# Two-layer hybrid decoder: the 64-row second score product and the 40-row bias broadcast on all 128 rows

## The chip, the cores and the metric

The program runs on one core of a Trainium2 chip, in one launch. Its metric is the device time in microseconds. Three runs of the kernel before took 1497.88, 1500.16 and 1502.87 us, so the median is 1500.16 us. Engines in the profile: PE is the matrix engine (its weight loads are shown apart, as PEld), DVE the vector engine, ACT the scalar engine, POOL the general engine, SP issues most DMAs.

## The reference, cut to what matters

The model is a trunk of two layers over 512 tokens of 1024 features in float32. Each layer has a mixer, a cross-attention into 256 memory tokens and a squared-ReLU MLP, each behind a norm and with a residual sum. The mixers hold three kinds of causal attention with heads of 64 features:

```python
# layer 0: forgetting attention, 8 heads
sc = einsum("bqhd,bkhd->bhqk", q, k) * 64 ** -0.5
bias = c[:, :, q0:q1, None] - c[:, :, None, :q1]        # c: running sum of log forget gates
p = softmax(where(mask, sc + bias, -inf)); out = p @ v
# layer 1: dilated attention, 8 heads, and sliding-window attention with sinks, 8 heads over 2 key heads
sc = einsum("nbqhgd,nbkhd->nbhgqk", qb, kb) * 64 ** -0.5 # only keys at allowed distances
num, m, den = p @ v, max(sc), sum(p)                     # then joined, divided by den
```

## The kernel before, in words

Activations lie with features on the 128 partitions and the 512 tokens in columns. To keep float32 accuracy every operand of a matmul is split in two: a first part, rounded by ACT into the type float32r, and the exact rest, which DVE gets by subtraction (hi_lo). A projection is then three matmuls for each block of 128 by 128 weights: first by first, first by rest, rest by first (mm3, lines 177 to 179). Weights come in chunks of 128x1024 by DMA, are split by ACT and DVE (lines 156 and 157) and are used once.

For the three causal attentions two heads share a tile of 128 features: head hh has rows 64 hh to 64 hh + 63. q_parts gives, for each head, a tile with the first part of q on the head's own rows and the rest of q on the other 64 rows. k_parts gives, for each head, a tile with the first part of k on both halves, and one tile for both heads with the rest of k, each head's on its own rows (line 385). A block of 128 queries then takes two products into one bank: the first (line 425) contracts over 128 rows and gives both parts of q by the first part of k; the second (line 426) contracts over the head's own 64 rows only and adds the first part of q by the rest of k.

The blocks of a head are done from the last to the first: 512, 384, 256 and 128 keys; in the window attention 256, 256, 256 and 128. Layer 0 adds a third product there, a mask on the diagonal block (line 428, bfloat16), and needs for each head the row of running sums on every partition: a product of a column of a selection matrix with the tile ch, which has the sums' first part on rows 0 to 7 and their rest on rows 32 to 39, 40 rows in all (line 683), copied out by ACT. So there are 96 second score products and 8 such broadcasts.

Behind the scores soft() runs: DVE adds the bias and finds the maximum (line 339), ACT takes the exponential and the sum (342), DVE the reciprocal (347), POOL scales (348). PE transposes the blocks (354), ACT and DVE split them (156, 157), and PE multiplies with V (448, 449).

The order of PE's instructions is written by merge(): the steps of the heads (scores of one head between the products with V of the one before) and the steps of projections, as filler, go into one list by their weight on PE and by estimates of when their inputs are ready. A score's weight there counts columns, not rows. The framework then places the buffers and adds the waits. Each pool gives a fixed number of buffers by tag: the tags acth and actl have eight each, and hold the gates and outputs of the layer 0 recurrence, the attention outputs and the rest of k, which takes one from either pool by turns.

Of the kernel before, what the change touches and what calls it, by code (L numbers as in the profile page):

```python
# [9 lines left out]
F32 = mybir.dt.float32  # L10
# [13 lines left out]
# columns of the small per-feature parameters  # L24
# [12 lines left out]
def build(ctx, tc, a):  # L37
# [53 lines left out]
    # the first weights come between the first blocks of x  # L91
# [15 lines left out]
    # the table of functions loads while the first data come  # L107
# [4 lines left out]
    # A step: (its weight on TensorE, function that emits it, what it needs, what it gives). merge() puts lists of  # L112
    # steps into one order: `ready` estimates when what a step gives can be used.
# [17 lines left out]
    def merge(*lists):  # L131
        """Each list stays in its order; of the steps that are ready goes the one whose list is furthest behind."""
        tot = [max(sum(s[0] for s in x), 1e-9) for x in lists]
        at = [0] * len(lists)
        done = [0.0] * len(lists)
        while True:
            left = [i for i in range(len(lists)) if at[i] < len(lists[i])]
            if not left:
                return
            when = {i: max([0.0, *(ready.get(x, 1e9) for x in lists[i][at[i]][2])]) for i in left}  # L140
            can = [i for i in left if when[i] <= now[0]]
            if can:
                i = min(can, key=lambda i: (done[i] + 0.5 * lists[i][at[i]][0]) / tot[i])
            else:
                i = min(left, key=lambda i: when[i])
                assert when[i] < 1e8, lists[i][at[i]][2]
            s = lists[i][at[i]]
            at[i] += 1
            done[i] += s[0]
            emit(s)  # L150

# [1 line left out]
    def hi_lo(hi, lo, src, scale=None):  # L153
        """src -> hi (12 bits) + lo (the exact rest)."""
        if scale is None:
            A.activation(out=hi, in_=src, func=AF.Copy)  # L156
            V.tensor_tensor(out=lo, in0=src, in1=hi.bitcast(F32), op=ALU.subtract)  # L157
        else:
            A.activation(out=hi, in_=src, func=AF.Copy, scale=scale)
            V.scalar_tensor_tensor(out=lo, in0=src, scalar=scale, in1=hi.bitcast(F32),  # L160
                                   op0=ALU.mult, op1=ALU.subtract)

    def chunk(src):
        """1024 columns of weights: the two parts."""
        cnt[0] += 1
        i = cnt[0]
        started.append(i)
        with tc.high_priority(100 if len(started) > 4 else 0):
            raw = wp.tile([128, 1024], F32, tag="wr", name=f"wr_{i}", bufs=2)
            h = wp.tile([128, 1024], F32R, tag="wh", name=f"wh_{i}", bufs=3)  # L170
            lo = wp.tile([128, 1024], F32R, tag="wl", name=f"wl_{i}", bufs=3)
            SY.dma_start(out=raw, in_=src)
            hi_lo(h, lo, raw)
        return h, lo
# [6 lines left out]
    def proj(src, xs, after, n=S, ks=range(8), need=(), give=(), bank=None):  # L181
        """Steps for one block of 128 output features; xs: list (filled by then) of (hi, lo) by block of the
        contraction. after(ps) follows the last."""
# [15 lines left out]
    def proj2(src, xs, k0, afters, need=(), banks=None):  # L199
        """A chunk with two blocks of output features; contraction over blocks k0 .. k0 + 3."""  # L200
        st = {}

        def f(e, k):
            def g():
                if "w" not in st:
                    st["w"] = [c.rearrange("p (e k m) -> p e k m", e=2, k=4) for c in chunk(src)]
                if k == 0:
                    st[e] = (banks[e] if banks else pmm)()
                h, lo = st["w"]
                x = xs[k0 + k]  # L210
                mm3(st[e], h[:, e, k, :], lo[:, e, k, :], x[0], x[1], k == 0, k == 3)
                if k == 3:
                    afters[e](st[e])
            return g

        return [step(0.65, f(e, k), need[k] if need else ()) for e in range(2) for k in range(4)]

    def proj_v(srcs, xs, out, nb, store, give=()):
        """By token: V of 512 features for nb blocks of tokens; store(b, ps) -> out"""
# [28 lines left out]
    class Stats:  # L248
        """The root of the mean square by token, of 8 blocks of features added one by one."""
# [25 lines left out]
        def last(self, src, c):  # L275
            """The last block's squares of columns c"""
# [8 lines left out]
        def rstd(self, b0=0, nb=None, more=()):  # L285
            """[128, nb], token = (b0 + b) * 128 + p; more: parts of squares of these tokens"""
# [17 lines left out]
    def spread(r, nb=4):  # L304
        """values by token -> the same row on every partition (PSUM)"""
# [29 lines left out]
    def soft(p, i, ps, bias, dens, sink=None):  # L335
        """scores (PSUM, unscaled) + bias -> exp(scores - max), and its sum"""
# [13 lines left out]
    def to_pt(blocks, n):  # L350
        """blocks: (source block [128, 128], column) -> transposed, in two parts"""
# [7 lines left out]
    def v_parts(t, src, scale=None):  # L359
        """Heads of 64 features -> for each its two parts side by side"""  # L360
# [4 lines left out]
    lows = [0]  # L365

    def q_parts(f):
        """Two heads on rows 0-63 and 64-127 -> for each a tile with both of its parts, the first on its own rows"""
# [7 lines left out]
    def k_parts(f):  # L376
        """For each head a tile with its first part twice; and the second parts"""
        x = (t2k("qkh", F32R), t2k("qkl", F32R))
        lows[0] += 1
        lo = t2k("acth" if lows[0] % 2 else "actl", F32R)  # L380
        for hh in range(2):
# [3 lines left out]
            V.tensor_tensor(out=lo[own, :], in0=f[own, :], in1=x[hh][own, :].bitcast(F32), op=ALU.subtract)  # L385
        return (*x, lo)
# [3 lines left out]
    def evac_head(y, hh, ps):  # L390
        """Rows 0-63 plus rows 64-127 -> rows hh * 64 .. of y"""
# [9 lines left out]
    class Head:  # L401
        """One head of causal attention on rows hh * 64 .. of the pair tiles: its steps."""
# [10 lines left out]
        def score(self, i):  # L413
# [6 lines left out]
            rows = slice(64 * self.hh, 64 * self.hh + 64)  # L420
# [4 lines left out]
            T.matmul(ps[:, :w], lhsT=q[hh][:, qc], rhs=k[hh][:, ks], start=True, stop=False)  # L425
            T.matmul(ps[:, :w], lhsT=q[hh][rows, qc], rhs=k[2][rows, ks], start=False, stop=self.mask is None)  # L426
# [26 lines left out]
        def steps(self, prev):  # L453
            """Its scores, between the previous head's products with V"""
# [29 lines left out]
    def out_half(src, ys, half, then=None, need=(), late=None):  # L484
        """hT += the half of the projection that belongs to ys[4 * half:]; a list of steps for each 2 blocks"""
# [10 lines left out]
    class Both:  # L496
        """Two lists of four as one, filled later"""
# [7 lines left out]
    def out_late(src, ys, half, gname, gi, hg, st):  # L505
        """The half whose last block comes late: (what can go before it, the rest)"""
# [10 lines left out]
    def mixer0():  # L517
# [12 lines left out]
        # softplus(-lam) = max(-lam, 0) + log1p(exp(-|lam|))  # L530
# [51 lines left out]
        def recur():  # L582
            for b in range(4):
                A.activation(out=gs[b], in_=gs[b], func=AF.Gelu_apprx_tanh)
            # a = exp(-8 r sp), kept as 1 - (1 - a): 1 - a = tanh(4 r sp) (1 + a); 1 - a^2 = (1 - a)(1 + a)
# [27 lines left out]
        # forget gates: rows 0-7 take the weights' first part, rows 8-15 the rest  # L613
# [37 lines left out]
        ch = cst.tile([40, S], F32R, tag="chdm", name="ch")  # L651
        G.memset(ch.bitcast(F32), 0.0)
        self_ = cst.tile([40, 8], F32, name="self")
        sel = cst.tile([40, 8], F32R, name="sel")
# [25 lines left out]
        def bias(head):  # L680
            def f():
                ps = psc()
                T.matmul(ps, lhsT=sel[:, head:head + 1].to_broadcast([40, 128]), rhs=ch, start=True, stop=True)
# [69 lines left out]
    Rm = cst.tile([128, MEM], F32, name="Rm")  # L753

    def mem_tiles():
        """The blocks of features, one after another"""
# [202 lines left out]
    def finish(src, hid, st):  # L959
        """The last block of features, half of the tokens after half, and the final norm"""  # L960
# [22 lines left out]
    def mixer1(hg, st):  # L983
# [39 lines left out]
        def rope(c, name, need=()):  # L1023
            """Its steps, and the step after the exchange of rows by DMA"""
# [6 lines left out]
        def v_proj(c, dst):  # L1031
            """V of 128 features: by feature, then transposed; its parts -> dst, a list of tiles"""
# [30 lines left out]
        # sliding window with sinks; a pair tile holds heads p and p + 4  # L1063
# [91 lines left out]
def _by_col(w):  # L1155
    """[1024, n] -> n/128 chunks [128, 8 * 128]: partition = row within a block of 128"""
# [4 lines left out]
def _by_row(w):  # L1161
    """[1024, 512] -> 4 chunks [128, 2 * 512]"""
# [3 lines left out]
def _by_half(w):  # L1166
    """[1024, 1024] -> 8 chunks [128, 2 * 4 * 128]: a half of the rows, two blocks of columns"""
# [7 lines left out]
def _consts():  # L1175
# [12 lines left out]
    sel = np.zeros((40, 8), np.float32)  # L1188
# [74 lines left out]
```

## Time and profile before

| | us |
|---|---|
| median of three runs | 1500.16 (1497.88 to 1502.87) |
| span of the profiled execution | 1501.8 |
| PE busy | 1472.9 |
| DVE busy | 873.2 |
| ACT busy | 673.3 |
| POOL busy | 158.6 |

The page gives the profiled execution by its span, from the first to the last instruction; it names no other time for it. Busy is the time in which at least one instruction of the engine ran. Matmuls overlap each other, so PE's busy time says that it hardly rests and not how fast it goes: for that one reads the distance from the start of one matmul to the start of the next in the timeline. The three causal attentions lie from about 110 to 215 us (layer 0) and from about 776 to 955 us (layer 1).

### The profile page before, as it was taken

The numbers are of one execution on the slowest core, as the hardware profiler recorded it, in microseconds if no ns is written. First come the engines' busy times: TensorE is split into PE (matmuls) and PEld (weight loads), VectorE is DVE, ScalarE is ACT, GpSimd is POOL, SyncE is SP. The second block draws the span as 40 slices with busy tenths as digits, with TensorE's granted clock in tenths as the row PEclk, the third lists the DMA queues.
The fourth block names the chain that finished last, engine by engine and source line by source line (L and its number), as shares of the span: only waits on it lengthen the run. The fifth ranks groups of instructions, "written<-read, shape, count | busy, mean of one in ns | idle before, by whom it ended". The sixth has DMA issues, their size and how long they took to land.

```text
span 1501.8 us, 18306 instructions
## 1 busy us (share of the span) xinstructions
PE 1472.9 (98%) x6912; PEld 1201.5 (80%) x6912; DVE 873.2 (58%) x1507; ACT 673.3 (45%) x1161; POOL 158.6 (11%) x172
## 2 busy tenths in 40 slices
PE   8999999999999999999999999999999999999996
PEld 5777777888888888888877777788888888888885
DVE  7786767555444444444568887766454444444543
ACT  3776654444431323324446866645343323142342
POOL 3002212000200000000212221300021000000002
PEclk9999999999999999999999999999999999999998
DMA  5222213432333333233232222144323333233331
GB/s 192 80 82 71 71 56 120 141 112 72 98 98 99 98 94 97 92 98 98 98 105 78 63 72 84 57 141 127 110 72 98 95 98 92 95 98 99 98 99 56
DMA packets 46233, 142.83 MB, mean 95 GB/s; under 512 B 5698, under 2 KB 11202, under 8 KB 46146
## 3 DMA queue, kind: packets, MB, share of 16 engines
q1 hardware_dynamic: 45058, 140.63, 30.8%
q8 instruction: 54, 0.88, 0.2%
q10 hardware_dynamic: 1088, 1.05, 0.2%
q14 instruction: 33, 0.27, 0.1%
HBM read 136.15 MB, written 2.10 MB: 92 GB/s over the span
## 4 chain that ended last, share of the span: by engine, by line
PE 91%; DVE 5%; ACT 2%; issue 1%; DMA 1%; POOL 0%; SPq 0%; DVEq 0%; ACTq 0%; POOLq 0%
PE mm L177 25%; PE mm L178 25%; PE mm L179 25%; PE t L354 2%; PE s L426 2%; PE s L425 1%; DVE wl L157 1%; PE pv L449 1%; PE pv L448 1%; PE mm L233 1%; PE mm L234 1%; PE s L177 1%; PE mm L235 1%; DVE hgl L160 1%; PE s L178 1%
## 5 line engine op out<-in xcount | busy, mean ns | idle before, releaser
L156 ACT ACTIVATE wh<-wr 128x1024 fp32r<-128x1024 f32 x246 | 260.3, 1059 | 564.9 <-PE mm L178 514.4
L157 DVE TENSOR_TENSOR wl<-wr,wh 128x1024 fp32r<-128x1024 f32 x246 | 302.2, 1229 | 248.3 <-ACT wh L156 241.1
L177 PE MATMUL mm<-hgh,wh 128*128 128x512 f32 x888 | 353.7, 398 | 0.8 <-DVE qkl L579 0.7
L178 PE MATMUL mm<-hgl,wh 128*128 128x512 f32 x888 | 349.2, 393 | 3.6 <-DVE hgl L160 3.6
L179 PE MATMUL mm<-hgh,wl 128*128 128x512 f32 x888 | 348.3, 392 | 0.0
L177 PE MATMUL mm<-acth,wh 128*128 128x512 f32 x504 | 198.3, 396 | 0.8 <-DVE hT L477 0.8
L178 PEld LDWEIGHTS mm<-hgl,wh 128*128 128x128 f32 x888 | 167.7, 189 | 37.4 <-DVE hgl L160 4.4
L177 PEld LDWEIGHTS mm<-hgh,wh 128*128 128x128 f32 x888 | 167.7, 189 | 37.3 <-DVE qkl L579 1.1
L179 PE MATMUL mm<-acth,wl 128*128 128x512 f32 x504 | 196.7, 390 | 0.0
L178 PE MATMUL mm<-actl,wh 128*128 128x512 f32 x504 | 196.6, 390 | 0.1
L179 PEld LDWEIGHTS mm<-hgh,wl 128*128 128x128 f32 x888 | 167.7, 189 | 35.1
L270 POOL TENSOR_TENSOR ssq<-ssq,sq 128x512 f32<-128x512 f32 (+1 forms) x48 | 72.0, 1501 | 982.6 <-ACT sq L258 982.0
L937 DVE TENSOR_TENSOR kv<-mm,Rt 128x512 f32<-128x512 f32 x56 | 38.7, 692 | 150.9 <-PE mm L179 150.9
L177 PEld LDWEIGHTS mm<-acth,wh 128*128 128x128 f32 x504 | 94.3, 188 | 21.2 <-ACT acth L156 1.4
L179 PEld LDWEIGHTS mm<-acth,wl 128*128 128x128 f32 x504 | 94.6, 188 | 19.8
L178 PEld LDWEIGHTS mm<-actl,wh 128*128 128x128 f32 x504 | 94.7, 188 | 19.2 <-DVE actl L157 0.7
L348 POOL TENSOR_SCALAR p<-p,den 128x256 f32<-128x256 f32 (+1 forms) x96 | 62.3, 652 | 288.3 <-DVE den L347 266.9
L177 PE MATMUL mm<-v,wh 128*128 128x256 f32 (+1 forms) x260 | 87.0, 334 | 0.0
L178 PE MATMUL mm<-v,wh 128*128 128x256 f32 (+1 forms) x260 | 86.9, 334 | 0.0
L179 PE MATMUL mm<-v,wl 128*128 128x256 f32 (+1 forms) x260 | 86.7, 333 | 0.0
L477 DVE TENSOR_TENSOR hT<-hT,mm 128x512 f32<-128x512 f32 x53 | 35.9, 683 | 53.8 <-PE mm L179 53.7
L156 ACT ACTIVATE pth<-t 128x128 fp32r<-128x128 f32 (+3 forms) x112 | 47.2, 434 | 39.7 <-PE t L354 39.0
(299 smaller groups left out, 2110.4 us busy)
## 6 DMA issues: line engine op xcount, KB each, us to landing
wr<-in_mlp_up SPq DMA_DIRECT2D x64, 512.0 KB, 3.6
wr<-in_mlp_down SPq DMA_DIRECT2D x64, 512.0 KB, 3.6
wr<-in_cd_w_in SPq DMA_DIRECT2D x18, 512.0 KB, 3.6
wr<-in_xa_q SPq DMA_DIRECT2D x16, 512.0 KB, 3.6
wr<-in_xa_k SPq DMA_DIRECT2D x16, 512.0 KB, 3.7
wr<-in_xa_v SPq DMA_DIRECT2D x16, 512.0 KB, 3.6
wr<-in_xa_w_o SPq DMA_DIRECT2D x16, 512.0 KB, 3.6
wr<-in_ab_w_in SPq DMA_DIRECT2D x15, 512.0 KB, 3.6
```

What stands on the lines that cost most here:

```text
L156: A.activation(out=hi, in_=src, func=AF.Copy)
L157: V.tensor_tensor(out=lo, in0=src, in1=hi.bitcast(F32), op=ALU.subtract)
L160: V.scalar_tensor_tensor(out=lo, in0=src, scalar=scale, in1=hi.bitcast(F32), op0=ALU.mult, op1=ALU.subtract)
L177: T.matmul(ps, lhsT=wh, rhs=xh, start=start, stop=False)
L178: T.matmul(ps, lhsT=wh, rhs=xl, start=False, stop=False)
L179: T.matmul(ps, lhsT=wl, rhs=xh, start=False, stop=stop)
L270: eng.tensor_tensor(out=self.ssq, in0=self.ssq, in1=q, op=ALU.add)
L348: G.tensor_scalar(out=p, in0=p, scalar1=dens[:, i:i + 1], scalar2=1.0, op0=ALU.mult, op1=ALU.mult)
L354: T.transpose(ps[:, c:c + 128], src, ident)
L426: T.matmul(ps[:, :w], lhsT=q[hh][rows, qc], rhs=k[2][rows, ks], start=False, stop=self.mask is None)
L477: V.tensor_tensor(out=hT[:, e, :], in0=hT[:, e, :], in1=ps, op=ALU.add)
L937: V.tensor_tensor(out=t, in0=ps, in1=Rt, op=ALU.mult)
```

## The change

The rest of k gets a tile for each head, with the head's rest on both halves of the rows, so that the second score product contracts over 128 rows: the weights are the whole tile of q parts, the same as in the first product, and the sum now also has the rest of q by the rest of k. For that k_parts takes a buffer of both tags each time, and DVE does four subtractions of 64x512 in it where it did two. The tiles ch and sel get 128 rows, of which those beyond 40 are zero, and the broadcast contracts over 128 rows. Comments and docstrings go as well.

```diff
     def k_parts(f):
         x = (t2k("qkh", F32R), t2k("qkl", F32R))
-        lows[0] += 1
-        lo = t2k("acth" if lows[0] % 2 else "actl", F32R)
+        lo = (t2k("acth", F32R), t2k("actl", F32R))
         for hh in range(2):
             own, other = slice(64 * hh, 64 * hh + 64), slice(64 - 64 * hh, 128 - 64 * hh)
             A.activation(out=x[hh][own, :], in_=f[own, :], func=AF.Copy)
             A.activation(out=x[hh][other, :], in_=f[own, :], func=AF.Copy)
-            V.tensor_tensor(out=lo[own, :], in0=f[own, :], in1=x[hh][own, :].bitcast(F32), op=ALU.subtract)
-        return (*x, lo)
+            for r in (own, other):
+                V.tensor_tensor(out=lo[hh][r, :], in0=f[own, :], in1=x[hh][own, :].bitcast(F32), op=ALU.subtract)
+        return x, lo
...
-            T.matmul(ps[:, :w], lhsT=q[hh][:, qc], rhs=k[hh][:, ks], start=True, stop=False)
-            T.matmul(ps[:, :w], lhsT=q[hh][rows, qc], rhs=k[2][rows, ks], start=False, stop=self.mask is None)
+            T.matmul(ps[:, :w], lhsT=q[hh][:, qc], rhs=k[0][hh][:, ks], start=True, stop=False)
+            T.matmul(ps[:, :w], lhsT=q[hh][:, qc], rhs=k[1][hh][:, ks], start=False, stop=self.mask is None)
...
-        ch = cst.tile([40, S], F32R, tag="chdm", name="ch")
+        ch = cst.tile([128, S], F32R, tag="chdm", name="ch")
         G.memset(ch.bitcast(F32), 0.0)
-        self_ = cst.tile([40, 8], F32, name="self")
-        sel = cst.tile([40, 8], F32R, name="sel")
+        self_ = cst.tile([128, 8], F32, name="self")
+        sel = cst.tile([128, 8], F32R, name="sel")
...
-                T.matmul(ps, lhsT=sel[:, head:head + 1].to_broadcast([40, 128]), rhs=ch, start=True, stop=True)
+                T.matmul(ps, lhsT=sel[:, head:head + 1].to_broadcast([128, 128]), rhs=ch, start=True, stop=True)
...
-    sel = np.zeros((40, 8), np.float32)
+    sel = np.zeros((128, 8), np.float32)
```

## Rows read from the trace of the kernel before

**Rows 1.** The page, part 1: busy us (share of the span) xinstructions.

```profile
PE 1472.9 (98%) x6912; PEld 1201.5 (80%) x6912; DVE 873.2 (58%) x1507; ACT 673.3 (45%) x1161; POOL 158.6 (11%) x172
```

**Rows 2.** Waits: who, for whom: us in total, times, longest us.

```profile
PEld s L426 <- issue: 12.4, 52, 0.4
...
PE s L683 <- DVE ch L677: 1.2, 1, 1.2
```

**Rows 3.** Timeline of PE, layer 0: start us, us, engine, line, out<-in, shapes.

```profile
198.35 0.27 PE L354 MATMUL t<-ident,p 128*128 128x128 f32 x1
198.55 0.50 PE L683 MATMUL s<-ch,sel 40*128 40x512 f32 x1
198.97 0.51 PE L425 MATMUL s<-qkl,qkl 128*128 128x512 f32 x1
199.41 0.50 PE L426 MATMUL s<-actl,qkl 64*128 64x512 f32 x1
199.84 0.23 PE L428 MATMUL s<-cmask,identb 128*128 128x128 bf16 x1
199.91 0.39 PE L354 MATMUL t<-ident,p 128*128 128x128 f32 x2
200.05 0.47 PE L177 MATMUL mm<-acth,wh 128*128 128x512 f32 x1
200.37 0.39 PE L178 MATMUL mm<-actl,wh 128*128 128x512 f32 x1
...
204.28 0.60 PE L354 MATMUL t<-ident,p 128*128 128x128 f32 x4
```

**Rows 4.** Timeline of PE, layer 1.

```profile
859.16 0.28 PE L449 MATMUL pv<-ptl,vd 128*128 128x256 f32 x1
859.28 0.28 PE L425 MATMUL s<-qkh,qkh 128*128 128x256 f32 x1
859.49 0.38 PE L426 MATMUL s<-actl,qkh 64*128 64x256 f32 x1
859.80 0.44 PE L354 MATMUL t<-ident,p 128*128 128x128 f32 x2
860.00 0.48 PE L177 MATMUL mm<-acth,wh 128*128 128x512 f32 x1
860.31 0.39 PE L178 MATMUL mm<-actl,wh 128*128 128x512 f32 x1
860.54 0.40 PE L179 MATMUL mm<-acth,wl 128*128 128x512 f32 x1
```

**Rows 5.** Windows: us, busy of PE, PEld, DVE, ACT, POOL, clock, DMA share, GB/s.

```profile
110.00:212.00 102.00, 101.94 (x479) 75.31 (x480) 71.39 (x179) 67.46 (x152) 24.66 (x40) 0.97 0.23 70
770.00:800.00 30.00, 30.00 (x138) 23.63 (x137) 21.42 (x58) 16.17 (x42) 5.92 (x8) 1.00 0.31 88
800.00:880.00 80.00, 79.98 (x396) 61.08 (x394) 70.90 (x218) 62.24 (x172) 22.81 (x35) 1.00 0.23 64
880.00:910.00 30.00, 30.00 (x137) 23.83 (x136) 19.76 (x41) 17.19 (x33) 3.69 (x6) 1.00 0.35 103
910.00:960.00 50.00, 49.89 (x240) 37.39 (x239) 38.61 (x98) 29.72 (x71) 11.03 (x16) 1.00 0.18 55
```

**Rows 6.** Line 385: count, ns min/median/max, first and last start, shapes.

```profile
L385 DVE TENSOR_TENSOR acth<-kv,qkh x5: 670/676/684, 82.6 to 927.9; 64x512 fp32r<-64x512 f32 x5
```

**Rows 7.** Timeline of DVE behind the first split of k; idle time in brackets.

```profile
86.53 0.69 DVE L591 SCALAR_TENSOR_TENSOR kv<-acth,kv 128x512 f32<-128x512 f32 x1 [2.00 <-ACT acth L590]
```

**Rows 8.** Windows of line 426 alone: us, PE and PEld busy (count), clock, DMA.

```profile
770.00:800.00 30.00, 2.93 (x8) 1.46 (x8) 1.00 0.31 88
800.00:880.00 80.00, 13.39 (x35) 6.40 (x35) 1.00 0.23 64
...
910.00:960.00 50.00, 6.54 (x16) 2.92 (x16) 1.00 0.18 55
```

**Rows 9.** Window behind the wait for the forget-gate sum, columns as in rows 5.

```profile
112.00:119.00 7.00, 7.00 (x20) 4.83 (x20) 5.09 (x16) 5.58 (x12) 1.45 (x2) 0.51 0.07 21
```

More of the change, by code (lines that the diff above doesn't have):

```diff
@@ L363, in v_parts @@
         hi_lo(o[:, :, 0, :], o[:, :, 1, :], src.rearrange("p (g c) -> p g c", g=g), scale)
-    lows = [0]
     def q_parts(f):
@@ L419, in score @@
             q, k = self.qk()
-            rows = slice(64 * self.hh, 64 * self.hh + 64)
             w, ks = self.w[i], slice(self.k0[i] * 128, self.k0[i] * 128 + self.w[i])
```

## The prediction

> **What bounds the kernel now.** I read the page's busy times first: PE is busy 1472.9 of 1501.8 us, DVE 873.2 [rows 1]. So the whole is a stream of matmuls; the question is only what a matmul costs in it. The view of waits says how little PE waits for others near the change: 1.2 us once, for the last part of the forget-gate sum, before the first bias broadcast; the weight loads of the second score product, on the other hand, stand idle 52 times, 12.4 us in all, for "issue", that is for nothing that another engine does [rows 2]. Then the timeline of PE, read by the distance from one start to the next. In plain work a product of 512 columns is followed by the next after 0.23 us (860.31 to 860.54), one of 256 after 0.12 (859.16 to 859.28); four transposes in a row end 0.60 after the first began and one takes 0.27, so they are 0.11 apart [rows 3, 4]. Around the products with fewer than 128 rows the distances are longer: 0.42 after the 40-row broadcast, 0.44 before and 0.43 after the 64-row product of 512 columns, 0.21 before and 0.31 after one of 256 columns [rows 3, 4]. The same 128 columns and dtype without the row change (first product, projections, products with V) show none of this. Last, busy time by stage, to see whom PE would wait for if it were faster [rows 5].
>
> **The change, part by part.**
>
> *64 rows become 128 (96 products).* Each keeps its columns, and if a full-row product runs at the plain distance, what goes is the excess. Layer 1, 256 columns, from the start of the product with V at 859.16 to the second projection product at 860.31: 1.15 us. At plain distances: 0.12 for it, 2 x 0.12 for the two score products, 2 x 0.11 for two transposes, 0.23 for the projection product, together 0.81. Excess 0.34 [rows 4]. The part behind the narrow product is 0.43 - 0.23 = 0.20 at 512 columns and 0.31 - 0.12 = 0.19 at 256 [rows 3, 4], so it hangs on the switch and not on the width, and I take 0.34 for all 64 scores of layer 1: 21.8 us.
>
> *40 rows become 128 (8 broadcasts).* Layer 0, first score of a head with its broadcast: from the transpose at 198.35 to the second projection product at 200.37 is 2.02 us. At plain distances: 0.11 for the transpose, 3 x 0.23 for the broadcast and the two score products, 0.11 for the mask product and the load behind it, 2 x 0.11, 0.23: 1.36. Excess 0.66 [rows 3], both narrow products together. The three other scores of a head have no broadcast and end in the mask product, whose cheap load takes up part of the exit (0.07 to the next start); I take 0.25 for each, between the 0.20 of the exit alone and the 0.34 of layer 1. A head: 0.66 + 0.75 = 1.41; eight heads: 11.3 us. So PE could give back 33.1 us in all.
>
> *More DVE work.* The key's split writes the second part for each head on both halves: 2 more subtractions of 64x512 per call, 9 calls, at 0.68 us [rows 6]: 12.2 us of DVE, and one more buffer for each call. The first call falls before the recurrence; behind its last subtraction DVE stands idle 2.00 us until an exponential of ACT is there [rows 7], and 1.36 us fit into that, so the chain to the forget-gate sum, which PE waits for, does not move. If that cover were gone, it would cost these 1.36 us once. The ACT work, all matmul counts and the loads stay.
>
> *Who is late next.* By stage [rows 5], PE's need after the change against DVE's:
> Layer 0 attention, 110 to 212: PE 102 - 11.3 = 90.7, DVE 71.39 + 3 x 1.36 = 75.5. PE stays the bound; all 11.3 us are kept.
> 770 to 800: 8 of the 64 scores [rows 8], 2.7 us; DVE 21.42 of then 27.3: kept.
> 800 to 880: 35 scores, 11.9 us, PE's need 68.1. DVE has 70.90 and gets 2 x 1.36 = 2.7 more (two of the calls): 73.6. DVE becomes the bound. At full use the stage takes 73.6 and gives 6.4; at the share that DVE has now (70.90 of 80, 0.886) it would take 83.1 and lose 3.1; if DVE's rest could be carried over into the next stage, which has 9 us of DVE to spare, all 11.9 would be given. I take 6.4, the middle one: queues of a few buffers carry some rest, and never all.
> 880 to 910: the 5 scores left, 1.7; DVE 19.76 + 1.36 = 21.1 of 28.3: kept.
> 910 to 960: 16 scores [rows 8], 5.4, PE's need 44.6; DVE 38.61 + 1.36 = 40.0, which at 0.886 takes 45.1, a gain of 4.9. I take 5.1.
> Layer 1: 2.7 + 6.4 + 1.7 + 5.1 = 15.9. With layer 0: 27.2 us. From the profiled 1501.8 that is 1474.6; the page gives the span alone and it lies among the runs shown (1497.88 to 1502.87), 1.6 above their median, so 1473 for a median.
>
> *The clock.* From 112 to 119 us the granted clock is 0.51, that is half of the time at the lower level, 1.2 GHz; before it PE had stood idle on the wait for the forget-gate sum [rows 2, 9]. That wait stays, so I keep the spell; without it about half of 7 us, 3.5, would be gained.
>
> *Buffers.* The second parts now take one buffer of each of two pools of eight, which also hold the attention outputs. In layer 0 when the last key pair is split: four outputs of the recurrence, two or three of attention, the key pair in use and the new one: eight. In layer 1: four window outputs, two others, two key pairs: eight. So it just fits, and I cost it at nothing.
>
> **A rule against the change.** The trace shows 0.43 us from a 64-row product of 512 columns to the next start, against 0.23 after a full one [rows 3]. The Trainium skill (TensorE: Matmul & The Clock Gate, section "Why this matters for your kernels") says that a single product with a contraction of 32 takes the same time as one with 128. By it alone padding rows would neither cost nor give anything, and the time would stay with the 12.2 us of DVE added. This case's rows differ from it, in a stream of full-row neighbours; the measurement decides, and the rule gets the small chance of the third rival.
>
> **The rivals.**
> 1. *PE alone decides.* DVE's rest is carried through the slack that its queue has, and all 33.1 us come: 1467 for a median. For it: PE hardly waits now though DVE is at 0.886 in the densest stage. Against: there is no room left there, 73.6 against 68.1.
> 2. *DVE keeps its share.* Its idle time in 800 to 880 is waiting inside the chain score, maximum, exponential, scaling, transpose, split, and does not shrink: that stage loses 3.1 instead of winning 6.4, the last gives 4.9: 27.2 - 9.5 - 0.2 = 17.5, some 1483 for a median. For it: a head's chain crosses DVE three times. Against: much of that idle time ends with a score from PE, which now comes sooner.
> 3. *The change doesn't do what it says.* The gaps belong to something else than the rows (the second product in a row on the same weights, say), and stay; with DVE's extra work hidden 1500, with a part of it in front of PE 1504. Against: projections have the same sequence of three products in one bank without a gap [rows 3, 4].
> 4. *Slower.* The pools run full: each of the 9 splits waits for a buffer, its pair's scores wait for it, PE stands some 4 us and then runs 3.4 us at the lower clock (half of the spell at 112 [rows 9]), 1.7 more: 9 x 5.7 = 51 us against the 33.1 gained, 1518. It decides from 33.1 / 9 = 3.7 us for a split. For it: the count of eight in eight. Against: the count does fit, and a buffer comes free each time that a pair's scores are done.
>
> **How the numbers follow.** Forecast 0.50, rival 1 0.20, rival 2 0.20, rival 3 0.04, rival 4 0.06. The forecast's own range is 1468 to 1479. The range goes down to rival 1 with a tenth more excess than the two samples show and the low spell of the clock shortened (1462), and up over rival 2 (1487). About 0.3% (4.5 us) is what a measurement of this kernel can tell from no change. Faster by more: 0.90; within it: 0.04; slower: 0.06.
>
> **What would show it.** In the profile after, all second score products and broadcasts are 128 rows, their weight loads no longer idle for "issue", and 0.23 (512), 0.12 (256) and 0.11 (128) us follow one another around them. The attention of layer 0 ends about 11 us earlier. In layer 1 DVE is at 0.95 or more where it was at 0.886, and PE shows waits for the split transposes or the scaled scores there. Wrong would be: gaps of 0.3 us and more left around the full-row products (rival 3); no new waits of PE (rival 1); DVE not above 0.9 with PE waiting (rival 2); PE waiting for the key's second parts, and a lower clock behind it (rival 4).

## The result, and the profile after

The changed kernel takes 1474.8 us (median of 4 runs, 1473.98 to 1476.31) against 1499.2 of the kernel before beside it (4 runs, 1497.88 to 1502.87): a ratio of 0.9836, 95% interval 0.9821 to 0.9852, so 24.4 us less. Its profiled execution has a span of 1474.4 us and a time of 1476.31, 1.9 above the span.

The page after, part 1, with the columns of [rows 1]:

```profile
PE 1441.2 (98%) x6912; PEld 1195.4 (81%) x6912; DVE 880.9 (60%) x1525; ACT 670.9 (45%) x1161; POOL 162.2 (11%) x172
```

As many matmuls as before, 31.7 us less of PE; 18 more instructions on DVE, which are the 18 subtractions added. Next the spot of [rows 3], the first score of a head in layer 0 with its broadcast (timeline of PE, after; lines 680, 422 and 423 are 683, 425 and 426 of before):

```profile
187.03 0.27 PE L354 MATMUL t<-ident,p 128*128 128x128 f32 x1
187.06 0.48 PE L680 MATMUL s<-ch,sel 128*128 128x512 f32 x1
187.38 0.39 PE L422 MATMUL s<-qkl,qkl 128*128 128x512 f32 x1
187.61 0.40 PE L423 MATMUL s<-actl,qkl 128*128 128x512 f32 x1
187.85 0.23 PE L425 MATMUL s<-cmask,identb 128*128 128x128 bf16 x1
187.91 0.39 PE L354 MATMUL t<-ident,p 128*128 128x128 f32 x2
188.06 0.48 PE L177 MATMUL mm<-acth,wh 128*128 128x512 f32 x1
188.37 0.39 PE L178 MATMUL mm<-actl,wh 128*128 128x512 f32 x1
```

From the transpose to the second projection product it is 1.34 us (187.03 to 188.37), where it was 2.02; the plain distances add up to 1.36. The spot of [rows 4], layer 1:

```profile
837.76 0.27 PE L446 MATMUL pv<-ptl,vd 128*128 128x256 f32 x1
837.87 0.28 PE L422 MATMUL s<-qkh,qkh 128*128 128x256 f32 x1
837.99 0.28 PE L423 MATMUL s<-acth,qkh 128*128 128x256 f32 x1
838.10 0.38 PE L354 MATMUL t<-ident,p 128*128 128x128 f32 x2
838.24 0.48 PE L177 MATMUL mm<-acth,wh 128*128 128x512 f32 x1
838.55 0.40 PE L178 MATMUL mm<-actl,wh 128*128 128x512 f32 x1
```

0.79 us (837.76 to 838.55) where it was 1.15. The five stages of [rows 5], cut at the same places in the count of PE's matmuls (windows of after, columns as there; before, they took 99.4, 23.5, 79.6, 31.0 and 49.4 us), and in the second row the stretch of [rows 9]:

```profile
108.00:194.80 86.80, 84.68 (x461) 68.86 (x460) 73.06 (x179) 64.53 (x148) 25.51 (x39) 1.00 0.26 77
112.00:119.00 7.00, 7.00 (x38) 5.49 (x37) 6.15 (x16) 6.56 (x15) 3.04 (x4) 1.00 0.39 88
762.80:783.70 20.90, 20.90 (x110) 17.39 (x109) 16.35 (x52) 13.12 (x38) 6.10 (x8) 1.00 0.36 102
783.70:857.10 73.40, 71.49 (x394) 58.09 (x392) 69.63 (x214) 60.30 (x167) 22.73 (x32) 1.00 0.25 69
857.10:886.40 29.30, 28.90 (x143) 23.99 (x143) 23.82 (x50) 19.09 (x40) 5.59 (x8) 1.00 0.39 110
886.40:932.20 45.80, 45.08 (x236) 36.51 (x235) 38.52 (x98) 28.86 (x70) 11.46 (x16) 1.00 0.20 57
```

In the densest stage (783.7 to 857.1) DVE is busy 69.63 of 73.40, a share of 0.95; before, between the same places, it was 0.89:

```profile
799.80:879.40 79.60, 79.58 (x394) 60.74 (x393) 70.68 (x216) 62.09 (x172) 22.65 (x34) 1.00 0.23 64
```

In 112 to 119 the granted clock is 1.00, the upper level of 2.4 GHz, where the profile before had 0.51.

The order of PE's matmuls is not quite the same in the two traces, though the change leaves merge() and its weights alone: some 130 of the 6912 stand at other places, most of them in the densest stage. Its end cuts through such a place, so the stage holds 0.8 us more of plain PE work after than before (six more products of 512 columns, four transposes and one product with V fewer), and the third stage as much less. The attention of layer 1 as a whole holds the same 875 matmuls in all kernels below but one (narrow product twice has more); it took 183.4 us before and takes 169.5 after.

To see where the time of PE went, I add up all distances from one matmul's start to the next and take off the plain ones: 0.227 us for 512 columns (ten products in a row from 783.43 to 785.70), 0.172 for 384, 0.117 for 256, 0.109 for a transpose and for the other products of 128 columns, 0.065 for a mask product. What is left is excess, either next to a second score product (with its broadcast and mask) or elsewhere (us):

```
                        next to second scores    elsewhere
stage                   before   after           before   after
layer 0, behind 119 us  10.4     0.5             1.9      3.1
first, 8 scores          2.4     0.2             0.7      0.3
densest, 35 scores      10.6     1.3             3.6      6.1
third, 5 scores          1.4     0.0             0.6      0.9
last, 16 scores          4.6     0.9             3.0      2.9
layer 1 together        19.0     2.4             7.9     10.2
```

At the scores of layer 1 16.6 us went; 2.3 net came back as longer distances elsewhere, with 2.5 in the densest stage. Ten of those gaps are over 0.15 us there, 3.7 us together (one of 0.2 before, and PE's waits named none there), and no two of the four that the waits name have the same releaser (waits of PE in 783.7 to 857.1, after; columns as in [rows 2]):

```profile
PE pv L445 <- DVE kv L395: 0.5, 1, 0.5
PE s L422 <- DVE nm L339: 0.4, 1, 0.4
PE t L354 <- DVE v L157: 0.4, 1, 0.4
PE pv L445 <- ACT pth L156: 0.3, 1, 0.3
```

### The profile page after: what moved, and what is told of

It reads as the page before. It is cut to its first block, busy times and chain, and to the rows that moved or that the text cites. A ratio compares the mean times of both kernels' runs of the same rounds, so it can differ in the third digit from the quotient of the medians.

```text
span 1474.4 us, 18320 instructions
## 1 busy us (share of the span) xinstructions
PE 1441.2 (98%) x6912; PEld 1195.4 (81%) x6912; DVE 880.9 (60%) x1525; ACT 670.9 (45%) x1161; POOL 162.2 (11%) x172
## 4 chain that ended last, share of the span: by engine, by line
PE 84%; DVE 8%; ACT 4%; issue 1%; DMA 1%; SPq 0%; POOL 0%; DVEq 0%; ACTq 0%; POOLq 0%
PE mm L178 24%; PE mm L177 24%; PE mm L179 24%; DVE wl L157 2%; PE t L354 1%; ACT wh L156 1%; PE s L177 1%; PE s L178 1%; PE s L179 1%; PE mm L234 1%; PE mm L233 1%; PE mm L235 1%; DVE hgl L160 1%; PE pv L446 1%; PE s L422 1%
## 5 line engine op out<-in xcount | busy, mean ns | idle before, releaser
L348 POOL TENSOR_SCALAR p<-p,den 128x256 f32<-128x256 f32 (+1 forms) x96 | 65.7, 689 | 255.5 <-DVE den L347 186.2
L179 PE MATMUL mm<-v,wl 128*128 128x256 f32 (+1 forms) x260 | 86.8, 334 | 0.0
L157 DVE TENSOR_TENSOR ptl<-t,pth 128x128 fp32r<-128x128 f32 (+3 forms) x112 | 53.2, 482 | 10.0 <-ACT pth L156 9.5
```

The costliest lines, as they stand in the source:

```text
L179: T.matmul(ps, lhsT=wl, rhs=xh, start=False, stop=stop)
L348: G.tensor_scalar(out=p, in0=p, scalar1=dens[:, i:i + 1], scalar2=1.0, op0=ALU.mult, op1=ALU.mult)
```

## The experiments

Ratios are to the kernel before, run on the same chip, with the 95% interval; "densest" is the length of the densest stage between the same two places in PE's count (79.6 before, 73.4 after), with DVE's busy share; "layer 1" is that of the whole attention of layer 1 (183.4 before, 169.5 after), which holds the same matmuls in each kernel listed with a number.

| kernel | median us | ratio | densest, DVE | layer 1 |
|---|---|---|---|---|
| broadcast alone | 1496.73 | 0.9984 (0.9975 to 0.9994) | 79.5, 0.89 | 183.4 |
| scores alone | 1478.57 | 0.9859 (0.9845 to 0.9873) | 73.5, 0.95 | 169.5 |
| narrow product twice | 1514.33 | 1.0090 (1.0059 to 1.0121) | |  |
| one rest tile | 1475.12 | 0.9842 (0.9829 to 0.9856) | 73.9, 0.95 | 169.8 |
| split written twice | 1486.20 | 0.9915 (0.9900 to 0.9931) | 77.3, 0.96 | 176.6 |
| sine product on POOL | 1481.77 | 0.9872 (0.9852 to 0.9893) | 76.1, 0.92 | 175.6 |
| one rest tile and POOL | 1482.84 | 0.9880 (0.9860 to 0.9900) | 76.7, 0.89 | 176.1 |
| no sine product | 1475.41 | 0.9828 (0.9805 to 0.9851) | 73.0, 0.91 | 169.5 |
| one rope product | 1475.56 | 0.9830 (0.9809 to 0.9852) | 74.0, 0.87 | 170.0 |
| later due times | 1482.67 | 0.9876 (0.9861 to 0.9890) | 74.9, 0.94 | 171.3 |
| one rest tile, later due | 1476.75 | 0.9838 (0.9821 to 0.9855) | 74.6, 0.93 | 170.3 |
| no sink term | 1475.88 | 0.9847 (0.9829 to 0.9866) | 72.7, 0.94 | 170.1 |

PE's order of matmuls is that of before in broadcast alone and, within layer 1, in one rest tile; in scores alone it is that of after. The other kernels differ from both, by some 130 to over 1000 places.

**The two parts, each alone.** Broadcast alone is the kernel before with the five places of 40 rows at 128; scores alone is the changed kernel with these five back at 40:

```diff
-        ch = cst.tile([40, S], F32R, tag="chdm", name="ch")
+        ch = cst.tile([128, S], F32R, tag="chdm", name="ch")
...
-                T.matmul(ps, lhsT=sel[:, head:head + 1].to_broadcast([40, 128]), rhs=ch, start=True, stop=True)
+                T.matmul(ps, lhsT=sel[:, head:head + 1].to_broadcast([128, 128]), rhs=ch, start=True, stop=True)
```

> The kernel before with the 40-row broadcast on 128 rows and nothing else. Theory (PE pays for each change of the number of rows, on the way in and on the way out): the distances behind the broadcast fall from 0.42 to 0.23 us and those before it from 0.20 to 0.11; 8 times about 0.3 us, 2.5 us in all, 1496.7 against 1499.2. Rival (only the 64-row products cost, a broadcast is too rare to matter): within 0.5 us of 1499.2.

> The kernel after with the broadcast left on 40 rows. Theory: all but the 2.5 us of the broadcast is gained, 1477.3, and the layer 1 attention takes what it takes in the kernel after. Rival (the half-speed spell at 112 us has gone because the broadcast no longer interrupts the stream): the spell is back, 3 us more, about 1480.

The broadcasts alone give 2.3 us, the scores alone 20.5. The first of the two shows both prices side by side (timeline of PE, broadcast alone, where line 683 is the broadcast and 426 still the narrow score):

```profile
193.32 0.48 PE L683 MATMUL s<-ch,sel 128*128 128x512 f32 x1
193.64 0.39 PE L425 MATMUL s<-qkl,qkl 128*128 128x512 f32 x1
193.96 0.50 PE L426 MATMUL s<-actl,qkl 64*128 64x512 f32 x1
194.39 0.23 PE L428 MATMUL s<-cmask,identb 128*128 128x128 bf16 x1
```

The full score product, with full-row neighbours ahead, is followed by the narrow one after 0.32, and the narrow one by the mask product after 0.43: 0.09 over 0.23 on the way in, 0.20 on the way out. In [rows 3], with the broadcast narrow too, the same full product had 0.44, 0.12 more, so a part of the broadcast's way out falls there. The profiles of both kernels have a granted clock of 1.00 through 112 to 119, so in scores alone the spell is not back, as the rival there had it.

**Narrowness or the switch?** The kernel before, with its narrow product issued twice:

```diff
-            T.matmul(ps[:, :w], lhsT=q[hh][rows, qc], rhs=k[2][rows, ks], start=False, stop=self.mask is None)
+            for e in range(2):
+                T.matmul(ps[:, :w], lhsT=q[hh][rows, qc], rhs=k[2][rows, ks], start=False,
+                         stop=self.mask is None and e == 1)
```

> The kernel before with each 64-row product done twice, one right behind the other (the rest of k is added twice). Theory (it is the change of the number of rows that costs, not a narrow product): from the first to the second narrow product the distance is the plain one, 0.23 us at 512 columns, 0.17 at 384, 0.12 at 256, 0.11 at 128, 13.9 us for 96 products, 1513. Rival (a narrow product costs more by itself): the second costs what the first does, 0.43, 0.37, 0.31 and 0.25 us, 31 us in all, 1530.

It takes 12.5 us more than before by the medians, near the 13.9 of the theory and far from the 31 of the rival. Its timeline of PE (x2: the two narrow products, given in one row) at 512 and at 256 columns:

```profile
200.62 0.73 PE L427 MATMUL s<-actl,qkl 64*128 64x512 f32 x2
201.28 0.23 PE L430 MATMUL s<-cmask,identb 128*128 128x128 bf16 x1
...
205.55 0.50 PE L427 MATMUL s<-actl,qkl 64*128 64x256 f32 x2
205.98 0.23 PE L430 MATMUL s<-cmask,identb 128*128 128x128 bf16 x1
```

Two take 0.66 us until the next start (200.62 to 201.28), one took 0.43 [rows 3]; at 256 columns two take 0.43 and one 0.31 [rows 4]. The second costs 0.23 and 0.12, the plain distances of full-row products. So a product of 64 rows is as quick as one of 128; what costs is to change the row count between one product and the next. The Trainium skill (TensorE: Matmul & The Clock Gate, section "Why this matters for your kernels") says that a single product of 32 rows takes the same time as one of 128. For the product itself these rows agree; for a single narrow product between full ones they differ, since it stands between two switches, and the measurement decides. The Trainium skill (TensorEngine Tiling (Array Packing), section "Key Properties") says that changing the tiling mode, though not the tile alone, drains TensorE. The 0.29 us for there and back would fit that; no row here shows the drain itself.

One rest tile, below, shows the price of the switch with the least else changed. In layer 1 its PE runs in the order of before, and DVE's instructions there add up to as much (168.5 us, 168.3 before); only the second score products have 128 rows. Layer 1 falls from 183.4 to 169.8 us.

**DVE's load: less, and more.** The forecast had the densest stage bound by DVE. One rest tile puts both heads' second parts of key into one tile, as the two heads' halves don't overlap: one subtraction per head as before the change, and a buffer fewer. Split written twice doubles the added work instead:

```diff
-        lo = (t2k("acth", F32R), t2k("actl", F32R))
+        lows[0] += 1
+        lo = t2k("acth" if lows[0] % 2 else "actl", F32R)
...
-            for r in (own, other):
-                V.tensor_tensor(out=lo[hh][r, :], in0=f[own, :], in1=x[hh][own, :].bitcast(F32), op=ALU.subtract)
-        return x, lo
+            V.tensor_tensor(out=lo[own, :], in0=f[own, :], in1=x[hh][own, :].bitcast(F32), op=ALU.subtract)
+        return x, (lo, lo)
```

```diff
-            for r in (own, other):
+            for r in (own, other, own, other):
```

> The kernel after, with one tile for the rest of k as before, both heads' rests in it, and the second product over all 128 rows of it: DVE does 18 subtractions of 64x512 less (12.4 us), and one buffer less is taken each time. The rest of q then meets the other head's rest of k, a term of the size of the product of two rests. Theory (DVE bounds the layer 1 attention now, busy 0.95 of its dense stage): PE's stalls there shrink by about the DVE work that goes from there, 4 us, 1471. Rival A (the stalls are the latency of the chain score, maximum, exponential, transpose, not DVE's load): no change, 1474.8. Rival B (the buffers are what delays): the gain shows at the splits of k and layer 0 gains as well.

> The kernel after with every subtraction of the split of k done twice, 36 more of 64x512 on DVE (24.7 us). Theory (DVE is the bound of the dense stage of layer 1 alone): some 8 us more in layer 1 (5.5 us of new DVE work in the dense stage and 5.5 in the two behind it, part of it in idle time), at most 2 us in layer 0, 1483 to 1485. Rival A (latency, not load): at most 2 us more, 1477.

More work costs: 11.4 us over the changed kernel, 7.1 of it in layer 1 (for 12.4 us of DVE's instructions there) and 3.8 in the densest stage, whose window again holds some 0.8 us more of plain PE work (windows of split written twice, that stage, then of one rest tile):

```profile
787.40:864.70 77.30, 73.70 (x393) 58.68 (x392) 73.88 (x218) 59.83 (x165) 24.11 (x32) 1.00 0.23 61
```

```profile
783.90:857.80 73.90, 71.14 (x394) 57.82 (x393) 69.96 (x216) 61.74 (x172) 24.90 (x34) 1.00 0.24 69
```

With the 18 subtractions gone the time stays. In the densest stage this is no test of the load, for the durations on DVE add up to 83.2 us there with one rest tile and to 82.8 in the changed kernel. But it shows no cost of the added subtractions in layer 1. Without them, and in the order of before, the distances elsewhere still grow by nearly 3 us. That buffers delay (rival B) doesn't show either: layer 0 takes 87.1 us, 86.8 in the changed kernel.

**A rope product off DVE, or gone.** Line 1016 multiplies by the rope's sine, 13 times in all (where an expectation below speaks of nine, that was miscounted). On POOL in place of DVE, in two kernels (the changed one, and one rest tile); left out; and with one product in place of the two and their sum:

```diff
-            V.tensor_tensor(out=swp, in0=swp, in1=sinR, op=ALU.mult)
+            G.tensor_tensor(out=swp, in0=swp, in1=sinR, op=ALU.mult)
```

```diff
-            V.tensor_tensor(out=swp, in0=swp, in1=sinR, op=ALU.mult)
```

```diff
-            V.tensor_tensor(out=raw, in0=raw, in1=cosR, op=ALU.mult)
-            V.tensor_tensor(out=swp, in0=swp, in1=sinR, op=ALU.mult)
-            V.tensor_tensor(out=raw, in0=raw, in1=swp, op=ALU.add)
+            V.tensor_tensor(out=raw, in0=raw, in1=Rt, op=ALU.mult)
```

> The kernel with one tile for the rest of k (18 subtractions less on DVE) and the product of the rotary embedding with the sines on POOL (9 of 128x512 less on DVE, five of them in the dense stage of layer 1). Theory (DVE's work in the dense stage sets its length, 73.85 us for 83.2 us of instructions there): 3.7 us less of DVE work there, 3.3 us less time, 1471.5. Rival A (latency of the head's chain): 1475. Rival B (POOL and DVE get into each other's way): DVE's instructions beside POOL's grow and eat the gain, 1475 or more.

> The kernel after with the product of the rotary embedding with the sines on POOL. Theory: DVE's dense stage loses 3.6 us of work as without the product, 1471 to 1472, as long as POOL, busy a fifth of the time there, has each done before its sum is due. Rival (POOL and DVE get into each other's way, or the longer way through POOL delays the keys): 1475 or more, while leaving the product out gains.

> The kernel after without the product of the rotary embedding with the sines (left out: the exchanged rows are added as they are). Nothing is put on another engine. Theory (DVE's work in the dense stage sets its length): five products of 0.72 us go from it, 3.6 us of 82.8; at the slope that the doubled split showed (3.84 us for 4.15 of work) 3.3 us less in that stage, and little in the others, 1471. Rival (latency of the head's chain, to which the rotary embedding does not belong): 1474 to 1475.

> The kernel after with one product in place of the two products and the sum of the rotary embedding (which is left out; q and k are scaled by the norm alone). In the dense stage of layer 1, 73.4 us in the kernel after, five products and six sums go, 8.0 of 82.8 us of DVE's instructions. Theory (DVE's load sets the length of that stage): it falls until PE's own need decides, to some 68.5 us, and the whole to 1470. Rival (not the load, but the order of the instructions and the latency of a head's chain: removing 3.6 us gave nothing): the stage stays over 72 us, the whole at 1473 to 1475.

On POOL it is slower by 7 and 8 us, against the theory of both expectations. The product takes 1296 ns there and 683 on DVE (line 1016 of sine product on POOL, then of after: count, ns min/median/max):

```profile
L1016 POOL TENSOR_TENSOR kv<-kv,sinR x13: 1277/1296/1804, 746.5 to 894.8; 128x512 f32<-128x512 f32 x13
```

```profile
L1016 DVE TENSOR_TENSOR kv<-kv,sinR x13: 661/683/889, 749.0 to 896.8; 128x512 f32<-128x512 f32 x13
```

The rival of POOL and DVE in each other's way can be checked at equal order, since the kernels with the sine product on POOL and without it have the same sequence of matmuls and, in the attention of layer 1, the same 401 DVE instructions. These add up to 166.1 us without the product and to 172.9 beside POOL's, and layer 1 takes 169.5 and 175.6 us. The longest cosine product of line 1015 goes from 934 to 1782 ns (sine product on POOL):

```profile
L1015 DVE TENSOR_TENSOR kv<-kv,cosR x13: 677/693/1782, 746.3 to 894.8; 128x512 f32<-128x512 f32 x13
```

So DVE's instructions do take longer beside POOL's; how much of the 6.1 us is that, and how much the longer way through POOL, stays open.

Without the sine product, and with one rope product, the time is that of the changed kernel, though DVE's share in the densest stage falls from 0.95 to 0.91 and 0.87 (windows of one rope product, that stage, then the waits of PE in it):

```profile
782.40:856.40 74.00, 71.54 (x394) 57.89 (x393) 64.66 (x209) 60.38 (x170) 21.85 (x34) 1.00 0.25 69
```

```profile
PE pv L445 <- ACT pth L156: 1.4, 3, 0.7
PE pv L446 <- DVE ptl L157: 0.6, 3, 0.2
```

Five us less of DVE (64.66 against 69.63), 0.6 us more of stage, and the waits are at other places: for ACT's first parts of the transposed scores now. Over the whole of layer 1 DVE's instructions add up to 173.2 us in the changed kernel, 166.1 without the sine product and 158.3 with one rope product; the stretch takes 169.5, 169.5 and 170.0 us. So there is no sign that DVE's load bounds this stage. PE's order moves with each of these edits, by 240 to 300 places, so a gain from the load that a worse order eats is not strictly excluded.

**The order, and the head's chain.** Two more candidates: the planner's estimates of when scaled scores and their transposes are there (6.5 and 2.5, raised to 9.0 and 3.5, in the changed kernel and in one rest tile), and the sink's exponential and its sum, which stand in each window head's chain:

```diff
-                      [(("P", self.name, i), 6.5), *(self.give_s if i == 0 else ())]) for i in (3, 2, 1, 0)]
+                      [(("P", self.name, i), 9.0), *(self.give_s if i == 0 else ())]) for i in (3, 2, 1, 0)]
...
-                      [(("T", self.name, j), 2.5)]) for j in (3, 2, 1, 0)]
+                      [(("T", self.name, j), 3.5)]) for j in (3, 2, 1, 0)]
```

```diff
-            es = small(1, tag="es")
-            A.activation(out=es, in_=sink[0], func=AF.Exp, bias=nm)
-            V.tensor_tensor(out=dens[:, i:i + 1], in0=dens[:, i:i + 1], in1=es, op=ALU.add)
+            pass
```

> The kernel after with longer estimates in the order of PE's work: scaled scores count as ready 9.0 us after their products (6.5 before), split transposes 3.5 us after theirs (2.5). Theory (PE waits for latency in an order that was made for the estimates): projections move between, the waits for score banks and split transposes in the dense stage go, and it falls from 73.4 to 70 or 71 us; 1471 to 1472. Rival (load): DVE has as much to do as before, the waits only move; 1474 to 1476.

> The kernel with one tile for the rest of k, with the same longer estimates (9.0 and 3.5 us). If the order is what holds the dense stage, it gains as much as the kernel after does from them, 1471 to 1472; if load and order hold it together, more than that, since DVE has 12.4 us less to do, 1469 to 1470; if neither, 1475.

> The kernel after without the sink's exponential and its sum into the denominator (left out of the window attention). Both stand inside the chain of a window head, between the exponential of a score and the reciprocal that POOL's scaling waits for: 24 times 0.28 us of ACT (6.8 us) and 24 times 0.17 us of DVE (4.1 us) in the dense stage. Theory now (what holds that stage is the way of a head from score to product with V, through the queues of DVE and ACT, and not DVE's load as such): the waits for split transposes and score banks shrink, the stage falls from 73.4 us to 71 or less, the whole to 1472. Rival A (the order, with its single bank for the products with V and two for the scores, holds it whatever the chain takes): over 73 us, 1474 to 1475. Rival B (ACT's load decides, 60.2 of 73 us): as the theory, but with ACT's share at or above its 0.82 and no slack left there.

Later due times cost 7.9 us, outside both its theory and its rival, some 4.5 of them in layer 0, where one score then waits 2.0 us for a bank that the maximum of an earlier score still holds (waits of PE in 108 to 200, later due times):

```profile
PE s L422 <- DVE nm L339: 2.2, 2, 2.0
```

Without the sink's instructions the densest stage is 0.8 us shorter, by as much plain PE work as its window holds less, and layer 1 and the whole are no shorter; the theory of the head's chain (71 us or less) fails too. With one rest tile the later due times cost 1.6 us. None of these kernels is measurably quicker than the changed one; one rest tile equals it with 18 subtractions and a buffer fewer.

## Why the prediction was right, and where it was not

The forecast was 1473 and the median is 1474.8. Its main mechanism holds: the excess hung on the change of rows, and the broadcasts and the second scores now run close to plain distances. Each part alone gives 20.5 and 2.3 us, 22.8 together. That the total came out so near is in part luck, as the steps show: the attention forecast at 27.2 us gave 9 in layer 0 and 14.0 in layer 1, some 23, and the rest of the difference is the clock's. Step by step:

*Layer 0* (11.3 forecast). At the spots it is right: behind 119 us alone 9.9 us went from the distances around narrow products. (The cut at 119 us is not at the same matmul in the two traces; it leaves 28 second scores before and 27 after.) But 1.2 us came back elsewhere, which I had cost at nothing because PE stays the bound there. It does; in one place the added subtractions stand ahead of a maximum all the same. DVE, then PE, in layer 0, after (idle time in brackets):

```profile
125.06 1.37 DVE L383 TENSOR_TENSOR acth<-kv,qkh 64x512 fp32r<-64x512 f32 x2
126.45 1.93 DVE L383 TENSOR_TENSOR actl<-kv,qkl 64x512 fp32r<-64x512 f32 x2
128.41 0.29 DVE L339 CUSTOM_DVE_ANT_0 p<-s,kv 128x128 f32<-128x128 f32 x1
```

```profile
127.60 0.48 PE L177 MATMUL mm<-acth,wh 128*128 128x512 f32 x1
128.86 0.47 PE L422 MATMUL s<-qkh,qkh 128*128 128x512 f32 x1 [0.78 <-DVE nm L339]
```

Four subtractions in a row, 3.3 us, two of them new; the maximum behind them holds a score's bank, and PE waits 0.78 us. With one rest tile, without the two new ones, that wait is gone, but one of 0.6 us for a split transpose is there in its place and the stage is no shorter (87.1 us). The stage is 12.6 us shorter than before, of which 3.4 are the clock's spell; 9 us are the change's.

*The first split of k*, cost at nothing under DVE's idle time [rows 7]: right. DVE's idle time there fell from 2.00 to 1.20 us, and the instruction behind it (line 588, 591 before) starts at 86.35, 86.53 before. The cover has an end: with the split written twice that instruction starts at 89.14, PE waits 2.29 us before the sums of the forget gates (1.1 in the changed kernel), and a spell at a granted clock of 0.5 follows, from about 104.5 to 108 us.

*Layer 1's excess* was the term most off: 0.34 us for each of 64 scores, 21.8, taken from one score of 256 columns. By the table above the excess was 19.0 in all, 0.30 a score, and 2.4 of it stays; 16.6 went. The 16 scores of 128 columns have less to lose, 0.21 each; the others have 0.32 to 0.34, as forecast.

*DVE becomes the bound of the densest stage* is the step whose reason is not borne out, though its numbers came out (6.4 forecast, 6.1 measured, DVE at 0.95); that they did is luck. By it 5.5 of 11.9 us were to be lost to DVE. What was there to win was 10.6, not 11.9; 1.3 of it stayed at the scores, and 2.5 came back at other places. That leaves 6.8, of which the stage shows 6.1, as its window now holds more plain work. Adding DVE work lengthens the stage (4.15 us of instructions, 3.8 us), but taking 2 to 5.5 us away (sums of DVE's durations 82.8 us after, 80.8 without the sine product, 77.3 with one rope product) doesn't shorten it by more than its window's plain work. A busy share of 0.95 was a fact; that it is a cause, no kernel shows. What PE meets is short queues: a maximum that frees a score's bank (after, PE and DVE):

```profile
798.13 0.40 PE L178 MATMUL mm<-hgl,wh 128*128 128x512 f32 x1
798.97 0.39 PE L422 MATMUL s<-qkl,qkl 128*128 128x256 f32 x1 [0.45 <-DVE nm L339]
```

```profile
796.99 0.69 DVE L371 TENSOR_TENSOR qkh<-kv,qkh 64x512 fp32r<-64x512 f32 x1
797.71 0.69 DVE L371 TENSOR_TENSOR qkl<-kv,qkl 64x512 fp32r<-64x512 f32 x1
798.43 0.48 DVE L339 CUSTOM_DVE_ANT_0 p<-s,sw,sink 128x256 f32<-128x256 f32 x1
```

The maximum is quick, but stands behind two splits of q in DVE's order. Before, PE came later to such places by 0.3 us for each score, and I take it that this covered them: its waits name none in that stage. Which of them go if DVE's order within a head is changed is open: the kernels above have their gaps at other places each. More buffers for scores, two of the eight tiles that PE writes to, were not tried.

*The last stage* (5.1 forecast): 3.5. The excess was 4.6 for 16 scores, and 0.9 of it stayed; nothing was lost elsewhere. *The two others* (2.7 and 1.7): 2.6 and 1.7, the second with some 0.8 us of plain work moved out of it into the densest stage.

*The clock's spell.* I kept it; the profile after doesn't have it. I also read its 0.51 as half of the time at the lower level, but the granted clock is 0.50 in 113 to 118, so nearly all of the 7 us were at 1.2 GHz; the cost of 3.4 us is the same. A single profile can't say whose the spell is: broadcast alone lacks it too, and so does narrow product twice, which has all the narrow products. The granted clock of whole executions says more. It is 0.993 or 0.994, as with the spell, in 18 of 36 executions of the kernel before, in 3 of 11 of broadcast alone and in 1 of 2 of narrow product twice, but in none of 42 of the kernels with full-row scores, which have 0.995 to 0.997. So low values go with the narrow scores, though not in each execution; why is open. At equal granted clock (0.995, 0.996, 0.997) the change is worth 23.1 to 23.4 us, so about 1 of the 24.4 us by the medians is the clock's. In the profiled spans, which differ by 27.4 (27.2 forecast), 3.4 are, as if every term had held. I also took the time as 1.6 under the span; it lies 1.9 above.

*The rivals.* PE alone decides: no, 2.3 us came back in layer 1. DVE keeps its share: no, it went from 0.89 to 0.95. The gaps belong to something else: no, they went with the rows, and a second narrow product has none. Slower by buffers: one rest tile, with a buffer fewer, takes the same time, and no wait of PE names the key's second parts.

## What to carry to other kernels

Count the places where a stream of matmuls changes its number of rows, price each there-and-back from start-to-start distances over all shapes that occur, not from one, and pad or group the narrow ones. An engine busy for 0.95 of a stage is not shown to bound it until work taken off shortens the stage: work added tells nothing, since an engine near full can become the bound when loaded. Before two kernels are compared by stage, compare the order of the matmuls in their traces: here an edit on DVE alone moved it. Take off the excess by place (at the edit, elsewhere) before and after; it says at once what was won and what came back.

## What was not expected

A switch of rows costs the same at 512 and at 256 columns (0.20 and 0.19 on the way out), and a second narrow product right behind the first costs only its plain 0.23 or 0.12 us. POOL's multiplication of 128x512 takes 1.30 us to DVE's 0.68, and giving it 13 of them made the kernel 7 us slower though DVE was the busier engine. The spell of half clock behind the forget-gate sum, 6.8 us, is in one profile alone, and the low clocks of whole executions that go with it did not come with any kernel whose scores all have 128 rows. PE's order of matmuls changed with edits that touch neither PE nor merge().
